# Six column groups of an SSD input projection with 512-column matmuls, and half of the gate columns moved one product later

## The chip, the core and the metric

The kernel runs on one core of a Trainium2 chip. The core has a matrix engine (TensorE, PE in the profile, with its weight loads shown apart as PEld), a vector engine (VectorE, DVE), a scalar engine (ScalarE, ACT), GpSimd (POOL, nearly unused here) and a queue (SyncE, SP) that issues the DMAs. Each engine works through its own queue in the order that was fixed when the program was built, and waits on semaphores for what others deliver. The metric is the device time of one launch in microseconds (us); less is better.

## What is computed

One sequence of 256 tokens passes through two layers of width 2048. Layer A is a Mamba-2 SSD mixer, layer B a dilated attention over keys and values made from layer A's output. In the reference, cut to layer A:

```python
shift, scale, gate = _adaln(c, ada_w[layer], ada_b[layer])
h = x * (1.0 + scale) + shift
proj = h @ in_w
z, xBC, dt = jnp.split(proj, [SSD_D_INNER, SSD_D_INNER + SSD_CONV_DIM], axis=-1)
xBC = jax.nn.silu(_causal_depthwise_conv(xBC, conv_w, conv_b))
xs, Bm, Cm = jnp.split(xBC, [SSD_D_INNER, SSD_D_INNER + SSD_BC_DIM], axis=-1)
...
y = _ssd_chunked(xs * dt[..., None], dt * A, Bm, Cm)
y = y + (xs * D_skip[:, None]).reshape(bsz, L, SSD_D_INNER)
y = y * jax.nn.silu(z.astype(jnp.float32))
...
return y @ out_w
...
x = _layer_norm(DEEPNORM_ALPHA * x + (1.0 + gate) * y, ln_g[layer], ln_b[layer])
```

`adaln` gives shift, scale and gate by the product of silu(c) with a matrix of 2048 x 6144. The input projection has 4096 columns for `z`, 4096 for `xs`, 1024 each for B and C, and 64 for `dt`. The heads fall into eight groups of 512 columns.

## The kernel before

**Precision.** Every operand of a large product is split in two: a high part, rounded to the type that the matrix engine multiplies, and the rest as a low part. Each product is the sum of high x high, high x low and low x high. `split` (L96) does that for a weight piece of 128 x 1024 numbers (512 KB): ACT copies `raw` to `whi` (L99), DVE subtracts to get `wlo` (L101). `load_piece` (L91) issues the DMA on SP; there are six `raw` buffers, and four each of `whi` and `wlo`. Layer A's input is kept as `hp` (L284), 128 x 2 x 16 x 256: first all 16 k tiles of the high part (`hhi`), then all of the low part (`hlo`).

**Forms of a product.** `cm_quad` (L132) makes 512 output columns, transposed, with the weights as the stationary operand: per piece two k tiles, per k tile and block of 128 columns three matmuls of 256 columns, in `cm_piece` (L125 to L127). Its four blocks share two PSUM tiles `acc`. `cm_wide` (L139), which layer B uses, makes 256 output columns: a high weight block is multiplied with both halves of the input side by side, 512 columns (L149), a low block with the high half, 256 columns (L152); the sums of the two halves lie next to each other in one `acc` tile per block, and are brought together by an ACT copy (L156) and a DVE addition (L157). `tm_chunk` (L181) makes 512 columns with tokens on the partitions (matmuls at L173 to L175). The pool `mm` holds four `acc` tiles in all.

**Layer A.** The input projection is cut into products named by kind and group: `bc` (B and C of two groups), `xs` and `z` of one group. Some of them are begun while h is still being made (`begun`, L310). In the loop at L628, turn g makes, in this order, `bc` of the next two groups (odd g), `xs` of group g + 1, the first SSD stage of group g (`stage1`), `z` of group g + 1, and the second SSD stage (`stage2`). Each of the four blocks of `xs` then passes `conv` (L316): ACT starts a sum (L320), DVE adds three shifted terms (L323), ACT applies SiLU (L325). For `xs` of groups 2 to 7 these read PSUM directly. Then follows the SSD output's product with `wout` in four parts of 512 columns (L720), 16 weight pieces each; under the first one y is transposed and split (`y_tiles`, L659). Each part ends with `residual` (L683), on DVE, which needs a piece of the gate row.

**The adaLN columns.** One column step loads 1 MB (`ada_load`, L242, tile `araw`, two buffers) and takes one DVE instruction of 2048 elements per partition (`ada_dot`, L251). `queue` (L267) puts such steps into the list `jobs`; each step also loads the next column. `background(n, every)` (L106) is called after every weight piece, and pops a job each time that its count reaches `every`. Layer A's 16 gate columns are queued in turn 1 of the loop, with one job for every five pieces (`R = (1, 5)`, L518), with `gate_out` (L258) behind them: bias, transpose on PE (L262), copy (L264), store to the DRAM row `gated` (L265). The first eleven columns for layer B are queued behind the first `wout` product (L727). `residual` reads the gate row by a broadcast DMA into `gt` (L730 and L731).

**Order.** The program is written as a sequence; a scheduler lays out each engine's queue by the written order and by when it expects operands and buffers to be ready, so an instruction can come ahead of its written place. Where the code has `tc.issue_after`, an instruction is held behind another on its engine.

Of the kernel before, what the change touches and what calls it, by code (L numbers as in the profile page):

```python
# [9 lines left out]
F32 = mybir.dt.float32  # L10
# [8 lines left out]
P = 128  # L19
L = 256  # L20
D = 2048
KT = D // P
# [24 lines left out]


@with_exitstack
def trunk(ctx, tc, xT, x, c, par, cst, bias, lnrow, ada, wdt, win, wout, wk, wv, wbin, wbout, out):  # L50
    nc = tc.nc
    V, S, T, PO = nc.vector, nc.scalar, nc.tensor, nc.gpsimd

# [82 lines left out]
            background(*rate)  # L136
        return ps

    def cm_wide(src, dst, rate=(0, 1)):  # L139


        ps = acc_pair()
        for q in range(KT // 4):
            hi, lo = (t.rearrange("p k n -> p (k n)").rearrange("p (k n) -> p k n", k=4)
                      for t in split(load_piece(src[q])))
            for k in range(4):
                kt = 4 * q + k
                for n in range(2):
                    T.matmul(ps[n], hi[:, k, n * P:n * P + P], xp[:, kt], start=kt == 0, stop=False,  # L149
                             skip_group_check=True)  # L150
                for n in range(2):
                    T.matmul(ps[n][:, 0, :], lo[:, k, n * P:n * P + P], xhi[:, kt, :], start=False, stop=kt == KT - 1,  # L152
                             skip_group_check=True)
            background(*rate)
        for n in range(2):
            S.activation(dst[:, n, :], ps[n][:, 1, :], AF.Copy)  # L156
            V.tensor_tensor(dst[:, n, :], ps[n][:, 0, :], dst[:, n, :], op=ALU.add)  # L157
# [132 lines left out]
    with ExitStack() as cA:  # L290
# [4 lines left out]
        def as_cm(t):  # L295
            return t.rearrange("p b n -> p (b n)").rearrange("p (i l) -> p i l", i=4)
# [8 lines left out]
        with ExitStack() as cS:  # L305
# [1 line left out]
            p0 = cS.enter_context(tc.tile_pool(name="p0", bufs=2))  # L307
            szt = [p0.tile([P, 2, 512], F32, name="sz") for _ in range(2)]

            begun = {("z", 0): (win[12], 6, szt[0]), ("z", 1): (win[13], 4, szt[1]),  # L310
                     ("xs", 1): (win[5], 4, as_cm(y[0])), ("bc", 2): (win[1], 4, as_cm(y[1])),
                     ("z", 2): (win[14], 14, y[2]), ("bc", 4): (win[2], 12, as_cm(y[3])), ("z", 4): (win[16], 6, y[4]),
                     ("bc", 6): (win[3], 12, as_cm(y[5])), ("z", 6): (win[18], 10, y[6]), ("z", 5): (win[17], 8, y[7])}
            xs, bc, sz = {}, {}, dict(enumerate(szt))

            def conv(ps, ct, dst):  # L316
# [24 lines left out]
            def hl_(kt):  # L341
                return hlo[:, kt, :]

            def product(kind, g, pre=None):

                src, k0, part = begun.get((kind, g), (None, 0, None))
                if src is None:
                    src = win[{"bc": g // 2, "xs": 4 + g, "z": 12 + g}[kind]]
                if kind == "z":
                    ps = tm_chunk(src, hh_, hl_, rate=R, k0=k0, pre=pre)  # L350
                    if g not in sz:
                        sz[g] = p0.tile([P, 2, 512], F32, name="sz")
                    for b in range(2):
                        if part is not None:
                            V.tensor_tensor(part[:, b, :], ps[b], part[:, b, :], op=ALU.add)
                        S.activation(sz[g][:, b, :], part[:, b, :] if part is not None else ps[b], AF.Silu)
                    return
                ps = cm_quad(src, hhi, hlo, rate=R, k0=k0)
                t = tiles(ps)
                if part is not None:  # L360
# [154 lines left out]
            aux = cS.enter_context(tc.tile_pool(name="aux", bufs=2, space=PSUM, reuse_waits="tile"))  # L515
            aux2 = cS.enter_context(tc.tile_pool(name="aux2", bufs=2, space=PSUM, reuse_waits="tile"))
            px = pe = cS.enter_context(tc.tile_pool(name="px", bufs=2, reuse_waits="tile"))
            R = (1, 5)  # L518


            scratch = wp1.tile([P, D], F32, name="araw")
# [106 lines left out]
            for g in range(G - 1):  # L628
                if g == 1:
                    pin[0] = latest[-1].ins  # L630
                    queue(wp1, [(0, "gate", kt) for kt in range(KT)])
                    jobs.append(lambda: gate_out(0))
                if g % 2 == 1:
                    product("bc", g + 1)
                product("xs", g + 1)
                if rs is not None:
                    stage3(g - 1, rs)
                st1 = stage1(g)
                if g < G - 2:
                    product("z", g + 1)  # L640
                rs = stage2(g, *st1)
# [71 lines left out]
        def first_weights(q):  # L713

            if q % 3 == 2 and q < 12:
                i = q // 3
                into = [slots.tile([P, 1024], F32R, name=f"s{2 * i + j}") for j in range(2)]
                first_v.append(split(load_piece(wv[2 * (i % 2)][i // 2]), into=into))

        for n in range(4):  # L720
            ps = tm_chunk(wout[n], lambda kt: yhi[kt // 16][:, kt % 16, :], lambda kt: ylo[kt // 4][:, kt % 4, :],
                          nk=2 * KT, rate=(1, 4) if n else (0, 1),
                          pre={0: y_ahead, 3: first_weights}.get(n), split_end=4 if n == 3 else 0)
            if n == 0:
                pin[0] = latest[-3].ins
                state[0] = 0
                queue(pn, cols1[:11])  # L727
            if n == 3:
                drain()
            gt = pn.tile([P, 512], F32, name="gt")  # L730
            bcast(gt, gated[0], 512 * n)  # L731
            for b in range(2):
                xr = pn.tile([P, 512], F32, name="xr", bufs=2)
                nc.sync.dma_start(xr, rows(x, b)[:, 512 * n:512 * n + 512])
                residual(n, ps[b], b, (gt, u[b][:, 512 * n:512 * n + 512]), xr)
                if n == 3:
# [86 lines left out]
    R = (0, 1)  # L823
# [192 lines left out]
def _dt(w):  # L1016

    a = np.zeros((2, 8, P, P), w.dtype)
    a[..., :64] = w.reshape(2, 8, P, 64)
    return a.transpose(0, 2, 1, 3).reshape(2, P, 1024)  # L1020


def _layout(x, c, ada_w, ada_b, ln_g, ln_b, a_in_w, a_conv_w, a_conv_b, a_dt_bias,
            a_A_log, a_D, a_norm_g, a_out_w, kv_w, b_in_w, b_out_w):
    f = np.float32
    par = np.zeros((P, NPAR), f)

# [36 lines left out]
    bc = np.stack([bb.reshape(D, G, P), cc.reshape(D, G, P)], 2).reshape(D, 2048)  # L1064
    win = _pieces(np.concatenate([bc, xs, z], 1))
    return {
        "xT": x[0].T.reshape(KT, P, L).transpose(1, 0, 2), "x": x[0], "c": c, "par": par, "cst": cst, "bias": bias,
        "lnrow": np.stack([ln_g[0], ln_b[0], ln_g[1], ln_b[1]]),
        "ada": ada, "wdt": _dt(dt), "win": win,
        "wout": _pieces(a_out_w[0]), "wk": _pieces(kv_w[:, :3072], 256, 4),  # L1070
        "wv": _pieces(kv_w[:, 3072:]), "wbin": _pieces(b_in_w[0], 256, 4), "wbout": _pieces(b_out_w[0]),
    }
# [20 lines left out]
```

## Time and profile before

| | |
|---|---|
| median of three runs | 1263.39 us (1263.02 to 1263.94) |
| the profiled execution | 1263.64 us, its span 1261.9 us |
| PE busy | 1225.5 us (97%) |
| DVE busy | 1023.6 us (81%) |
| ACT busy | 697.8 us (55%) |
| DMA | 335.92 MB, mean 266 GB/s |

All times inside the profile count from the start of the span. The busy time of an engine is the union of its instructions; matmuls are pipelined, so a matmul's shown length overlaps the next one, and distances between starts tell its price. "<-" in a wait names what ended it. The SSD loop with the rest of the input projection ends near 530 us; the four `wout` products follow.

### The profile page before, as it was taken

How to read it: one execution, taken by the hardware profiler on the slowest of the kernel's cores; microseconds unless marked ns; L12 is line 12 of the kernel's file. 1: busy time of each engine (PE TensorE's matmuls, PEld its weight loads, DVE VectorE, ACT ScalarE, POOL GpSimd, SP SyncE). 2: the span in 40 equal slices, each digit the busy share in tenths (PEclk: the TensorE clock that was granted, in tenths of full speed). 3: DMA queues.
4: the chain of work that ended last, by engine and by line, in shares of the span. 5: the costliest groups of instructions: out<-in, count | busy, mean ns of one | idle time of the engine just before them, and what ended most of it. 6: DMA issues, size and time to landing. Idle time of an engine off the chain costs nothing.

```text
span 1261.9 us, 19472 instructions
## 1 busy us (share of the span) xinstructions
PE 1225.5 (97%) x7470; PEld 1065.7 (84%) x7470; DVE 1023.6 (81%) x1442; ACT 697.8 (55%) x1017; POOL 0.2 (0%) x4
## 2 busy tenths in 40 slices
PE   4999999999999999999999999999999999999997
PEld 4889999899899989778888788888887888888886
DVE  6999986999998977869766579788888866758777
ACT  3655577857678876854344444334345644445631
POOL 0000000000000000000000000000000000000000
PEclk9999999999999999999999999999999999999999
DMA  9999968696876446568988469989998774364741
GB/s 379 422 421 423 420 237 282 217 338 252 311 272 216 161 152 208 184 213 315 322 286 280 151 189 350 359 331 343 355 381 324 247 238 149 120 196 132 227 179 66
DMA packets 80589, 335.92 MB, mean 266 GB/s; under 512 B 9104, under 2 KB 9328, under 8 KB 67696
## 3 DMA queue, kind: packets, MB, share of 16 engines
q1 hardware_dynamic: 80496, 334.69, 73.7%
q8 instruction: 58, 0.95, 0.3%
q14 instruction: 35, 0.29, 0.1%
HBM read 332.47 MB, written 2.18 MB: 265 GB/s over the span
## 4 chain that ended last, share of the span: by engine, by line
PE 80%; DVE 9%; DMA 6%; ACT 2%; issue 2%; SPq 0%; DVEq 0%; ACTq 0%
PE acc L149 13%; PE acc L175 12%; PE acc L174 12%; PE acc L173 12%; PE acc L127 7%; PE acc L125 7%; PE acc L152 7%; PE acc L126 6%; DMA araw<-in_ada 3%; DVE wlo L101 2%; DVE araw L251 2%; DVE cacc L323 1%; DMA raw<-in_wk 1%; DMA pT<-in_lnrow 1%; PE py L613 1%
## 5 line engine op out<-in xcount | busy, mean ns | idle before, releaser
L99 ACT ACTIVATE whi<-raw 128x1024 fp32r<-128x1024 f32 x392 | 411.6, 1058 | 376.6 <-PE acc L175 125.0
L101 DVE TENSOR_TENSOR wlo<-raw,whi 128x1024 fp32r<-128x1024 f32 x392 | 474.2, 1223 | 148.6 <-ACT whi L99 144.6
L149 PE MATMUL acc<-actT,whi 128*128 128x512 f32 x896 | 284.2, 397 | 0.0
L174 PE MATMUL acc<-wlo,actT 128*128 128x512 f32 x688 | 269.8, 392 | 1.0 <-DVE wlo L101 0.8
L173 PE MATMUL acc<-whi,actT 128*128 128x512 f32 x688 | 266.9, 394 | 0.5 <-ACT actT L670 0.5
L125 PE MATMUL acc<-actT,whi 128*128 128x256 f32 x768 | 218.2, 286 | 17.6 <-ACT actT L402 17.5
L251 DVE SCALAR_TENSOR_TENSOR araw<-araw,cb__72 128x2048 f32<-128x2048 f32 x96 | 219.6, 2288 | 17.5 <-DMA araw<-in_ada 17.4
L127 PE MATMUL acc<-actT,wlo 128*128 128x256 f32 x768 | 215.9, 286 | 5.8 <-DVE wlo L101 5.8
L126 PE MATMUL acc<-actT,whi 128*128 128x256 f32 x768 | 217.7, 285 | 0.0
L152 PEld LDWEIGHTS acc<-actT,wlo 128*128 128x128 f32 x896 | 166.8, 188 | 43.2 <-DVE wlo L101 5.6
L152 PE MATMUL acc<-actT,wlo 128*128 128x256 f32 x896 | 178.1, 280 | 2.1 <-DVE wlo L101 1.7
L175 PE MATMUL acc<-whi,actT 128*128 128x512 f32 x432 | 168.8, 391 | 0.0
L125 PEld LDWEIGHTS acc<-actT,whi 128*128 128x128 f32 x768 | 148.5, 194 | 19.3 <-ACT actT L402 17.7
L174 PEld LDWEIGHTS acc<-wlo,actT 128*128 128x128 f32 x688 | 129.3, 188 | 28.9 <-DVE wlo L101 3.3
L127 PEld LDWEIGHTS acc<-actT,wlo 128*128 128x128 f32 x768 | 147.2, 194 | 7.1 <-DVE wlo L101 6.6
L173 PEld LDWEIGHTS acc<-whi,actT 128*128 128x128 f32 x688 | 128.7, 188 | 26.6 <-ACT actT L670 1.2
L126 PEld LDWEIGHTS acc<-actT,whi 128*128 128x128 f32 x768 | 148.9, 194 | 0.3
L149 PEld LDWEIGHTS acc<-actT,whi 128*128 128x128 f32 x896 | 137.4, 189 | 0.2
L175 PE MATMUL acc<-whi,ylo 128*128 128x512 f32 x256 | 100.2, 392 | 0.0
L175 PEld LDWEIGHTS acc<-whi,actT 128*128 128x128 f32 x432 | 81.1, 188 | 16.7
L175 PEld LDWEIGHTS acc<-whi,ylo 128*128 128x128 f32 x256 | 48.0, 188 | 9.7
L323 DVE SCALAR_TENSOR_TENSOR cacc<-acc,prm,cacc 128x253 f32<-128x253 f32 (+2 forms) x96 | 42.1, 477 | 4.6 <-ACT cacc L320 4.4
(253 smaller groups left out, 1051.9 us busy)
## 6 DMA issues: line engine op xcount, KB each, us to landing
araw<-in_ada SPq DMA_DIRECT2D x96, 1024.0 KB, 7.7
raw<-in_win SPq DMA_DIRECT2D x160, 512.0 KB, 5.5
raw<-in_wout SPq DMA_DIRECT2D x64, 512.0 KB, 4.7
raw<-in_wbin SPq DMA_DIRECT2D x64, 512.0 KB, 4.3
raw<-in_wv SPq DMA_DIRECT2D x48, 512.0 KB, 5.7
raw<-in_wk SPq DMA_DIRECT2D x48, 512.0 KB, 8.3
cbc<-cumd SPq DMA_DIRECT2D x16, 512.0 KB, 5.4
raw<-in_wbout SPq DMA_DIRECT2D x16, 512.0 KB, 4.1
```

The costliest lines, as they stand in the source:

```text
L99: copied.append(S.activation(hi, raw, AF.Copy))
L101: latest.append(V.tensor_tensor(lo, raw, hi.bitcast(F32), op=ALU.subtract))
L125: T.matmul(o, hi[:, k, c_], ahi[:, kt, :], start=first, stop=False, skip_group_check=True)
L126: T.matmul(o, hi[:, k, c_], alo[:, kt, :], start=False, stop=False, skip_group_check=True)
L127: T.matmul(o, lo[:, k, c_], ahi[:, kt, :], start=False, stop=kt == k1 - 1, skip_group_check=True)
L149: T.matmul(ps[n], hi[:, k, n * P:n * P + P], xp[:, kt], start=kt == 0, stop=False, skip_group_check=True)
L152: T.matmul(ps[n][:, 0, :], lo[:, k, n * P:n * P + P], xhi[:, kt, :], start=False, stop=kt == KT - 1, skip_group_check=True)
L173: T.matmul(o, h_, hi[:, k, :], start=kt == k0, stop=False, skip_group_check=part)
L174: T.matmul(o, h_, lo[:, k, :], start=False, stop=False, skip_group_check=part)
L175: end = T.matmul(o, l_, hi[:, k, :], start=False, stop=kt == k1 - 1, skip_group_check=part)
L251: V.scalar_tensor_tensor(raw, raw, 1.0, cb_, op0=ALU.mult, op1=ALU.mult, accum_out=mod[layer][:, ct, j:j + 1])
L323: V.scalar_tensor_tensor(acc[:, o:], ps[:, :L - o], w[:, j:j + 1], acc[:, o:], op0=ALU.mult, op1=ALU.add)
```

## The change

Two parts of layer A change. First, `xs` of groups 2 to 7 is made by `cm_wide`, twice per group with 256 columns each, from weights that lie in an array of their own (`wxs`, pieces of 512 KB that hold four k tiles of 256 columns). `cm_wide` gets its moving operand as a parameter: `hp[:, :, kt, :]` for both halves, two runs of 256 columns. Each of its four results lies in SBUF in the tile `xs`, and `conv` works on it in place; the first two blocks of a group are convolved as soon as the first half of the product is done. `win` loses these columns, so the index of the `z` columns in it moves down by six.

Second, of the 16 gate columns the first eight stay in the SSD loop, with one job for every ten pieces; the other eight and `gate_out` are queued ahead of the first `wout` product, in the pool `pn`, with one job for every two pieces, and what is left of them is drained behind that product, ahead of its residual.

```diff
-    def cm_wide(src, dst, rate=(0, 1)):
+    def cm_wide(src, dst, rate=(0, 1), moving=None):
+        both, high = moving or (lambda kt: xp[:, kt], lambda kt: xhi[:, kt, :])
...
-                    T.matmul(ps[n], hi[:, k, n * P:n * P + P], xp[:, kt], start=kt == 0, stop=False,
+                    T.matmul(ps[n], hi[:, k, n * P:n * P + P], both(kt), start=kt == 0, stop=False,
...
-                    T.matmul(ps[n][:, 0, :], lo[:, k, n * P:n * P + P], xhi[:, kt, :], start=False, stop=kt == KT - 1,
+                    T.matmul(ps[n][:, 0, :], lo[:, k, n * P:n * P + P], high(kt), start=False, stop=kt == KT - 1,
...
+            def xs_wide(g):
+                xs[g] = p0.tile([P, 4, L], F32, name="xs")
+                for w in range(2):
+                    t = xs[g][:, 2 * w:2 * w + 2, :]
+                    cm_wide(wxs[2 * g - 4 + w], t, rate=R, moving=(lambda kt: hp[:, :, kt, :], hh_))
+                    for n in range(2):
+                        conv(t[:, n, :], 4 * g + 2 * w + n, t[:, n, :])
+
             def product(kind, g, pre=None):
+                if kind == "xs" and g > 1:
+                    return xs_wide(g)
...
-            R = (1, 5)
+            R = (1, 10)
...
-                    queue(wp1, [(0, "gate", kt) for kt in range(KT)])
-                    jobs.append(lambda: gate_out(0))
+                    queue(wp1, [(0, "gate", kt) for kt in range(KT // 2)])
...
+        state[0] = 0
+        queue(pn, [(0, "gate", kt) for kt in range(KT // 2, KT)])
+        jobs.append(lambda: gate_out(0))
         for n in range(4):
             ps = tm_chunk(wout[n], lambda kt: yhi[kt // 16][:, kt % 16, :], lambda kt: ylo[kt // 4][:, kt % 4, :],
-                          nk=2 * KT, rate=(1, 4) if n else (0, 1),
+                          nk=2 * KT, rate=(1, 4) if n else (1, 2),
                           pre={0: y_ahead, 3: first_weights}.get(n), split_end=4 if n == 3 else 0)
             if n == 0:
+                drain()
                 pin[0] = latest[-3].ins
...
-    win = _pieces(np.concatenate([bc, xs, z], 1))
+    win = _pieces(np.concatenate([bc, xs[:, :1024], z], 1))
...
+        "ada": ada, "wdt": _dt(dt), "win": win, "wxs": _pieces(xs[:, 1024:], 256, 4),
```

Left out are the new argument `wxs` of `trunk`, the renumbering of `win` in `begun` and `product`, and unchanged lines.

More of the change, by code (lines that the diff above doesn't have):

```diff
@@ L49, in trunk @@
 @with_exitstack
-def trunk(ctx, tc, xT, x, c, par, cst, bias, lnrow, ada, wdt, win, wout, wk, wv, wbin, wbout, out):
+def trunk(ctx, tc, xT, x, c, par, cst, bias, lnrow, ada, wdt, win, wxs, wout, wk, wv, wbin, wbout, out):
     nc = tc.nc
@@ L308, in trunk @@
             szt = [p0.tile([P, 2, 512], F32, name="sz") for _ in range(2)]
-            begun = {("z", 0): (win[12], 6, szt[0]), ("z", 1): (win[13], 4, szt[1]),
+            begun = {("z", 0): (win[6], 6, szt[0]), ("z", 1): (win[7], 4, szt[1]),
                      ("xs", 1): (win[5], 4, as_cm(y[0])), ("bc", 2): (win[1], 4, as_cm(y[1])),
-                     ("z", 2): (win[14], 14, y[2]), ("bc", 4): (win[2], 12, as_cm(y[3])), ("z", 4): (win[16], 6, y[4]),
-                     ("bc", 6): (win[3], 12, as_cm(y[5])), ("z", 6): (win[18], 10, y[6]), ("z", 5): (win[17], 8, y[7])}
+                     ("z", 2): (win[8], 14, y[2]), ("bc", 4): (win[2], 12, as_cm(y[3])), ("z", 4): (win[10], 6, y[4]),
+                     ("bc", 6): (win[3], 12, as_cm(y[5])), ("z", 6): (win[12], 10, y[6]), ("z", 5): (win[11], 8, y[7])}
             xs, bc, sz = {}, {}, dict(enumerate(szt))
@@ L342, in hl_ @@
                 return hlo[:, kt, :]
+            def xs_wide(g):
[5 more added lines that the diff above has]
+                        conv(t[:, n, :], 4 * g + 2 * w + n, t[:, n, :])
             def product(kind, g, pre=None):
+                if kind == "xs" and g > 1:
+                    return xs_wide(g)
                 src, k0, part = begun.get((kind, g), (None, 0, None))
                 if src is None:
-                    src = win[{"bc": g // 2, "xs": 4 + g, "z": 12 + g}[kind]]
+                    src = win[{"bc": g // 2, "xs": 4 + g, "z": 6 + g}[kind]]
                 if kind == "z":
@@ L1068, in _layout @@
         "lnrow": np.stack([ln_g[0], ln_b[0], ln_g[1], ln_b[1]]),
-        "ada": ada, "wdt": _dt(dt), "win": win,
+        "ada": ada, "wdt": _dt(dt), "win": win, "wxs": _pieces(xs[:, 1024:], 256, 4),
         "wout": _pieces(a_out_w[0]), "wk": _pieces(kv_w[:, :3072], 256, 4),
```

## The prediction

> **What bounds the kernel now.** I read the page's head and its chain first, then the busy time of each engine by stage, then the waits of TensorE in layer A, and last the order of single instructions around the change.
>
> ```profile
> span 1261.9 us, 19472 instructions
> ...
> PE 80%; DVE 9%; DMA 6%; ACT 2%; issue 2%; SPq 0%; DVEq 0%; ACTq 0%
> ```
>
> ```profile
> 236.00:400.00 164.00, 161.36 (x1285) 150.09 (x1284) 158.84 (x242) 121.50 (x197) 0.00 (x0) 1.00 0.79 281
> 400.00:531.50 131.50, 128.45 (x1035) 114.89 (x1033) 109.87 (x196) 101.03 (x169) 0.00 (x0) 0.99 0.54 179
> 531.50:581.00 49.50, 49.32 (x242) 39.58 (x242) 38.71 (x63) 29.33 (x48) 0.00 (x0) 1.00 0.71 239
> 581.00:625.00 44.00, 44.00 (x195) 36.43 (x195) 34.34 (x34) 16.99 (x16) 0.00 (x0) 1.00 0.94 343
> ```
>
> The columns are the stretch, its length, then busy time of PE, PEld, DVE, ACT and POOL, the granted clock, the DMA share and GB/s. From 236 to 531.5 us (SSD loop, the rest of the input projection) PE is busy 289.8 of 295.5 us. It sets the end here. But DVE is busy 158.84 of 164 us in the first of these stretches: it could not follow a much faster PE. The third row is nearly the first product of the SSD output (`wout[0]`), the fourth the second one.
>
> ```profile
> PE acc L127 <- DVE wlo L101: 3.8, 3, 2.1
> ```
>
> That is the longest entry among PE's waits between 216 and 531.5 us: three waits for the low half of a weight split, 3.8 us in total, one of 2.1 us. So two things can be won in this stage: matmul time itself, and a few microseconds behind DVE.
>
> **The matmuls of groups 2 to 7.** Before, each of the 16 k tiles of a group takes 12 matmuls of 256 columns; after, 4 of 512 and 4 of 256 (hi weights against h's halves side by side, lo weights against the high half). The columns, 3072, stay. Both forms stand in the trace, the second in layer B's projections.
>
> ```profile
> 302.11 0.28 PE L125 MATMUL acc<-actT,whi 128*128 128x256 f32 x1
> ...
> 314.59 0.28 PE L127 MATMUL acc<-actT,wlo 128*128 128x256 f32 x1
> ```
>
> ```profile
> 804.62 0.63 PE L149 MATMUL acc<-actT,whi 128*128 128x512 f32 x2
> 805.09 0.39 PE L152 MATMUL acc<-actT,wlo 128*128 128x256 f32 x2
> ...
> 814.37 0.63 PE L149 MATMUL acc<-actT,whi 128*128 128x512 f32 x2
> ```
>
> Starts are what count, since the ends are modelled. From 302.11 to 314.59 there are 104 steps: 0.120 us for 256 columns. From 804.62 to 814.37 there are 14 k tiles of two column blocks: 0.696 us for each. A group took 192 x 0.120 = 23.04 us and will take 32 x 0.696 = 22.28 us: 0.76 us less, **4.5 us** for six groups.
>
> One thing differs from layer B: there both halves of a k tile lie side by side, here they are two runs of 256 columns far apart in `hp`. No row shows such a moving operand. Bounds: nothing, or at most that the break costs as much as a second matmul, which makes 512 columns 0.240 us and the gain nil. I take nothing, because the 0.120 us repeat for every instruction of 256 columns, whatever it reads, and so look like a price of the instruction.
>
> The Trainium skill ("TensorE: Matmul & The Clock Gate", section Back-to-back issue gap) puts an isolated warm gap at N/2.4 + 2.5 ns, 109 ns for 256 columns and 216 ns for 512; the trace has 120, and 0.47/2 = 235 ns. By the page 64 matmuls fewer are worth 0.16 us per group, an estimate of 1.0 us in all. The measurement decides, but that result stands below as a rival.
>
> **What the wide form adds.** Each of 24 column blocks (4 in each of six groups) gets an ACT copy out of PSUM and a DVE add, rows of layer B:
>
> ```profile
> L156 ACT ACTIVATE s<-acc x20: 364/380/384, 797.9 to 900.2; 128x256 f32<-128x256 f32 x20
> ```
>
> ```profile
> L157 DVE TENSOR_TENSOR s<-acc,s x20: 414/418/428, 799.2 to 900.6; 128x256 f32<-128x256 f32 x20
> ```
>
> ACT: 24 x 0.380 = 9.1 us; it has 295.5 - 222.5 = 73 us idle in the stage, so nothing on the path. DVE: 24 x 0.418 = 10.0 us. In the stretch to 400 us not even half of that would fit, if nothing left it (5.1 us idle). Weight pieces stay at 8 of 512 KB per group, so splits and DMAs are as many as before; the smaller `win` and the new `wxs` cost nothing, since the same bytes arrive by the same queue. PSUM: the two halves of a group take the four `acc` banks in turn, two at a time; the first half's banks are asked for again only after the second half, 11.1 us later. The tightest case is behind group 2, where `z` 2 has a single piece left, and there the add has to wait for two blocks only, where before the next product waited for convolutions reading PSUM. I cost it at nothing; without that cover it is one eviction, 0.8 us.
>
> **What leaves the SSD loop.** Eight of the 16 gate columns.
>
> ```profile
> L251 DVE SCALAR_TENSOR_TENSOR araw<-araw,cb__72 x16: 2283/2291/2303, 239.4 to 398.6; 128x2048 f32<-128x2048 f32 x16
> ```
>
> That is 8 x 2.29 = 18.3 us off DVE, and 8 MB off SP's queue. The net on DVE in the stage is 10.0 - 18.3 = -8.3 us. The sixteen ran between 239 and 401 us, well ahead of the pace that the rate of 1 in 5 writes down (the last is called in product `z` 7), so the new rate of 1 in 10 will not space them either: the eight will come early, and the relief falls after about 310 us. The early waits, 1.7 of the 3.8 us, I leave in place.
>
> **The stall at 472 us.** This is where the order of the convolutions matters. Chain of waits, then the stretches around it:
>
> ```profile
> 460.57 2.33 DVE cacc L323 x6
> ...
> 471.36 1.15 DVE wlo L101
> 472.50 0.04 issue
> 472.55 0.39 PE acc L127
> ```
>
> ```profile
> 472.00:474.00 2.00, 1.46 (x10) 1.46 (x11) 2.00 (x3) 1.99 (x2) 0.00 (x0) 0.90 0.70 262
> 474.00:476.00 2.00, 2.00 (x11) 2.00 (x11) 2.00 (x4) 1.44 (x5) 0.00 (x0) 0.50 0.84 274
> 476.00:478.00 2.00, 2.00 (x15) 2.00 (x15) 1.39 (x3) 1.84 (x4) 0.00 (x0) 0.75 0.83 281
> ```
>
> Behind group 6's product DVE has four convolutions (12 steps of 2.33/6 = 0.39 us) beside the SSD work of group 5, and reaches the next low half late. PE stands 2.1 us, and then the granted clock falls: 2 x 0.10 + 2 x 0.50 + 2 x 0.25 = 1.7 us more. In the wide form the first two blocks are convolved under the second half's matmuls, and only two convolutions and two adds remain behind the product: 6 x 0.39 - 2 x 0.418 = 1.5 us less DVE work ahead of that weight. The wait shrinks to some 0.6 us, and the clock may hold. Bounds: the whole 3.8 us, or a loss of 1 us if the adds queue elsewhere as these did. I take **2.5 us** gained.
>
> The Trainium skill ("TensorE: Matmul & The Clock Gate", section Why this matters for your kernels) has the clock fall only after an idle gap of more than about 3 us; here it fell after 2.1 us. By the page a new stall of 2 us would cost only itself, by the trace 3.8 us; the trace decides.
>
> **What comes into the first SSD output product.** Eight columns (one per two weight pieces), then the gate's bias, transpose, copy, store, and the first broadcast of the gate row.
>
> ```profile
> L251 DVE SCALAR_TENSOR_TENSOR araw<-araw,cb__72 128x2048 f32<-128x2048 f32 x3 | 6.9, 2289 | 0.0
> ```
>
> DVE's group of that name between 531.5 and 581 us: three columns of layer 1, which now come later. DVE's room there is 49.5 - 38.71 + 6.9 = 17.7 us, the newcomers take 18.3: full to 0.6 us. In the next stretch it has 9.7 us left, enough for the three.
>
> ```profile
> 528.05 0.42 SPq L244 DMA_DIRECT2D araw<-in_ada  x1
> ...
> 537.26 0.42 SPq L244 DMA_DIRECT2D araw<-in_ada  x1
> ```
>
> ```profile
> araw<-in_ada SPq DMA_DIRECT2D x96, 1024.0 KB, 7.7
> ...
> gt<-gated SPq DMA_DIRECT2D x4, 256.0 KB, 6.0
> ```
>
> ```profile
> DMA to landing us min/median/max: 1.3/2.3/3.3
> ```
>
> ```profile
> 581.50 1.28 DVE L685 TENSOR_TENSOR u<-acc,gt 128x512 f32<-128x512 f32 x2
> ...
> 585.09 2.35 DVE L101 TENSOR_TENSOR wlo<-raw,whi 128x1024 fp32r<-128x1024 f32 x2
> ```
>
> The landing times belong to the store of the gate row; the last two rows are the residual of this product, which starts when PE is done with it, and the first low half behind it. The two column buffers of this pool were first loaded at 528 and 537 us; a buffer then needs 7.7 + 2.3 + 0.4 = 10.4 us per turn. The eighth column, fourth in the second buffer, ends at 537.3 + 3 x 10.4 + 10.0 = 578.5 us. The transpose comes behind the product on PE, near 581; half a microsecond later, copied, the row goes out, and is back in `gt` at 581.5 + 2.3 + 6.0 = 590 us. So the residual starts some 8 us later than at 581.50, and DVE runs in order: low halves for the second product stand behind it. The one at 585.09 is the fourth piece's; its matmuls are due three pieces (12 matmuls at 0.235 = 2.8 us each) after 581, at 589.4. If the order leaves it behind the late residual, it is ready at 590 + 3.6 + 1.2 = 594.8: 5.4 us of stall, and 1.7 for the clock. If two more splits go ahead of the residual, nothing is lost. Bounds 0 and 7.1 us. SP waits too, for the copied row and for the store; weights behind it are up to six loads ahead and cover that. I take **2.5 us** lost, nearer to zero, because the order is made with the loads' times counted in.
>
> **Sum.** -4.5 - 2.5 + 2.5 = -4.5 us on the profiled execution's 1263.64 us (span 1261.9): 1259.1. That execution stands 0.25 us above the median of the runs, so the forecast is 1258.9 us.
>
> **Rivals.**
>
> A, no matmul time is won (the two runs count as two matmuls, or the gap is the page's, which leaves 1.0 us): -2.5 + 2.5 to -1.0 on top, 1262.4 to 1263.4 us, taken as 1262.9. For it: no row has the operand. Against: 0.120 us in hundreds of rows.
>
> B, slower: the transpose of the gate columns holds PE. It is one instruction in PE's queue; if the order expects the eighth column earlier than it lands, all matmuls behind it stand.
>
> ```profile
> 455.71 0.27 PE L262 MATMUL aux<-cc,mod 128*16 128x128 f32 x1
> ```
>
> ```profile
> DVE araw L251 <- DMA araw<-in_ada: 17.4, 13, 7.0
> ```
>
> For it: in the old order this transpose, written behind product `z` 7, ran at 455.7 us, so it does go ahead of its place; and DVE does wait for columns expected too early. Against: without the 7.0 us at the very start these are 12 waits of 0.9 us. If each load were counted a third short of its 7.7 us, the fourth in its buffer would be expected 4 x 2.6 = 10.3 us early; with 1.7 for the clock, in place of the 2.5: -7.0 + 12.0 = +5.0, 1268.4 us. It decides from 7.0 us on.
>
> C, DVE becomes the bound of the SSD loop: the early eight columns with the adds of groups 2 to 4 fill 158.84 + 5.0 of 164 us before any relief, and PE gives back what it won; the stall at 472 us, after the relief, still shrinks: 1263.4 - 2.5 + 2.5 = 1263.4 us. For it: that stretch's row. Against: the columns are placed where DVE is idle, and eight fewer come.
>
> **Chances.** A difference of 0.2% (2.5 us) is about what a measurement of this kernel can tell from no change. Forecast 0.62 (own range 1254.5 to 1261.5; all but 0.04 of it faster), A 0.08 (no change), C 0.13 (0.08 no change, 0.03 slower, 0.02 faster), B 0.17 (slower, but 0.02). Faster 0.60, no change 0.22, slower 0.18. The range runs from all of the stall's 3.8 us won and nothing lost (1263.4 - 8.3 = 1255.1) to short of B's price, 1265.5, with half a microsecond below for waits that I left in place.
>
> **What would show it.** Right: L125, L126 and L127 at 384 matmuls each, L149 and L152 at 1280, 0.696 us per k tile in the new rows; the loop's end near 524 us instead of 531.5; no half clock near 470 us; column dots between 536 and 579 us. Wrong: 512-column starts 0.24 us apart or more; PE's longest wait at L262 or behind L685; DVE over 97% from 236 to 500 us.

## The result and the profile after

The changed kernel takes 1254.7 us (median of six runs, 1252.97 to 1255.17) beside 1262.69 us for the kernel before on the same chip (six runs, 1261.64 to 1263.94). The ratio is 0.9935 [0.9925, 0.9946]: 8.0 us faster. The forecast was 4.5 us faster; the measured time lies in the range, near its lower end.

The page's head and the chain that ended last, of the changed kernel:

```profile
span 1252.5 us, 18746 instructions
...
PE 86%; DVE 5%; DMA 5%; issue 2%; ACT 1%; SPq 0%; DVEq 0%; ACTq 0%
```

PE's share of the chain rose from 80 to 86%, DVE's fell from 9 to 5%: the chain is the same, with fewer pieces in which PE waits for DVE. The stretches, with borders that follow the earlier end of the loop (columns as before):

```profile
236.00:400.00 164.00, 164.00 (x1092) 142.22 (x1091) 152.84 (x253) 127.40 (x216) 0.00 (x0) 1.00 0.69 239
400.00:522.50 122.50, 119.16 (x840) 99.32 (x838) 108.66 (x191) 99.14 (x172) 0.00 (x0) 1.00 0.54 178
522.50:572.00 49.50, 49.17 (x243) 39.76 (x244) 47.63 (x75) 29.37 (x49) 0.00 (x0) 1.00 0.92 332
572.00:616.00 44.00, 44.00 (x197) 36.32 (x196) 34.94 (x35) 16.99 (x16) 0.00 (x0) 1.00 0.95 360
```

In the first stretch PE has no idle time left, where it had 2.64 us. In the third, DVE is busy 47.63 of 49.50 us with the late gate columns, and PE is busy 49.17 us of it (49.32 before). PE's longest wait for DVE between 216 and 523 us, of those after:

```profile
PE acc L152 <- DVE wlo L101: 2.1, 1, 2.1
```

So the early waits are gone, and a wait of 2.1 us is there as before (it starts near 465 us). One wait has grown, for ACT, at the start of the first output product; before and after:

```profile
PE acc L173 <- ACT actT L670: 0.3, 1, 0.3
PE acc L173 <- ACT actT L681: 1.2, 1, 1.2
```

It comes with the wide form: it stands at 1.2 us in every profile that has it, and isn't there with the moved columns alone. Why ACT is later there wasn't tried. The starts of the wide form's matmuls, from PE's timeline in group 7:

```profile
445.05 0.63 PE L149 MATMUL acc<-actT,whi 128*128 128x512 f32 x2
...
449.23 0.63 PE L149 MATMUL acc<-actT,whi 128*128 128x512 f32 x2
```

Six k tiles of two blocks in 4.18 us: 0.697 us for each, as in layer B. The two runs of 256 columns far apart cost nothing that this shows.

**Where the time came from.** The loop is best added up over PE's records: from the first matmul of `stage2` of group 0 (L604 before, L616 after) to the first transpose of y (L666, L677). "Matmuls" is the number of instructions of each kind by its distance between starts; "idle" is the time without any matmul record; "half clock" is half the time for which the profile shows the granted clock at 0.50. All in us, one line per profiled execution; the experiments' rows are used further down.

```
kernel, execution        length  matmuls  idle  half clock  waits of PE over 0.3 us, and when
before                    297.9   287.2    5.1     1.7      1.35 @246, 0.42 @253, 0.88 @373, 2.08 @472, 0.37 @516
before, again             296.2   287.2    4.9     0        1.38 @248, 0.45 @254, 0.65 @374, 2.08 @474, 0.37 @516
changed                   288.8   282.7    2.1     0        2.08 @467
changed, again            290.3   282.7    2.1     1.7      2.08 @467
changed, third            288.8   282.7    2.1     0        2.08 @467
without the late eight    288.8   282.7    2.1     0        2.07 @467
wide form alone           294.5   282.8    6.0     1.7      1.38 @247, 0.97 @289, 2.67 @295, 1.03 @473
wide form alone, again    295.4   282.8    6.7     1.7      1.40 @247, 0.97 @289, 2.68 @295, 0.62 @376, 1.03 @474
moved columns alone       296.6   287.1    3.1     3.4      2.61 @508, 0.51 @509
moved columns, again      295.4   287.1    3.4     1.7      2.62 @507, 0.74 @509
all sixteen late          288.8   282.7    2.1     0        2.07 @469
split ahead               287.1   282.7    0.5     0        0.49 @469
ahead and held            287.2   282.7    0.5     0        0.50 @469
```

The loop became 9.1 us shorter between the two first executions: 4.5 of matmuls, 3.0 of idle time, 1.7 of half clock. The span became 9.4 us shorter, so on balance nearly all of it is in the loop; behind it, 1.7 us of half clock in the kernel before (near 716 us) stand against the longer wait for ACT, 0.9 us, and small differences in the rest. (The 3.9 to 4.0 us that the terms leave over are starts that come later than the usual distance, with no time free of a matmul record; they are the same in both. Without any use of the distances, as length less idle time and half clock, the loop went from 291.1 and 291.3 us in the two profiles before to between 286.5 and 286.7 in the three after.)

### The profile page after: what moved, and what is told of

Its sections match the earlier page's. It is cut to its first block, busy times and chain, and to the rows that moved or that the text cites. A ratio compares the mean times of both kernels' runs of the same rounds, so it can differ in the third digit from the quotient of the medians.

```text
span 1252.5 us, 18746 instructions
## 1 busy us (share of the span) xinstructions
PE 1218.5 (97%) x7086; PEld 1042.7 (83%) x7086; DVE 1032.4 (82%) x1466; ACT 702.1 (56%) x1039; POOL 0.2 (0%) x4
## 4 chain that ended last, share of the span: by engine, by line
PE 86%; DVE 5%; DMA 5%; issue 2%; ACT 1%; SPq 0%; DVEq 0%; ACTq 0%
PE acc L149 20%; PE acc L174 13%; PE acc L175 13%; PE acc L173 13%; PE acc L152 10%; PE acc L125 3%; PE acc L127 3%; PE acc L126 3%; DMA raw<-in_wk 2%; DVE wlo L101 1%; PE py L625 1%; DMA raw<-in_win 1%; DVE araw L251 1%; DMA araw<-in_ada 1%; DMA raw<-in_wv 1%
## 5 line engine op out<-in xcount | busy, mean ns | idle before, releaser
L149 PE MATMUL acc<-actT,whi 128*128 128x512 f32 x1280 | 405.2, 397 | 0.0
L152 PE MATMUL acc<-actT,wlo 128*128 128x256 f32 x1280 | 253.7, 280 | 4.5 <-DVE wlo L101 3.7
L149 PEld LDWEIGHTS acc<-actT,whi 128*128 128x128 f32 x1280 | 195.8, 189 | 0.4
L125 PE MATMUL acc<-actT,whi 128*128 128x256 f32 x384 | 108.9, 288 | 17.6 <-ACT actT L414 17.5
L126 PE MATMUL acc<-actT,whi 128*128 128x256 f32 x384 | 109.5, 287 | 0.0
L127 PE MATMUL acc<-actT,wlo 128*128 128x256 f32 x384 | 107.3, 287 | 1.2 <-DVE wlo L101 1.2
L125 PEld LDWEIGHTS acc<-actT,whi 128*128 128x128 f32 x384 | 74.3, 194 | 18.6 <-ACT actT L414 17.7
L126 PEld LDWEIGHTS acc<-actT,whi 128*128 128x128 f32 x384 | 75.1, 196 | 0.3
L583 ACT ACTIVATE seg<-cbc,cumT 128x128 f32<-128x128 f32 x128 | 41.2, 389 | 5.0 <-PE py L625 4.9
```

The costliest lines, as they stand in the source:

```text
L125: T.matmul(o, hi[:, k, c_], ahi[:, kt, :], start=first, stop=False, skip_group_check=True)
L126: T.matmul(o, hi[:, k, c_], alo[:, kt, :], start=False, stop=False, skip_group_check=True)
L127: T.matmul(o, lo[:, k, c_], ahi[:, kt, :], start=False, stop=kt == k1 - 1, skip_group_check=True)
L149: T.matmul(ps[n], hi[:, k, n * P:n * P + P], both(kt), start=kt == 0, stop=False, skip_group_check=True)
L152: T.matmul(ps[n][:, 0, :], lo[:, k, n * P:n * P + P], high(kt), start=False, stop=kt == KT - 1, skip_group_check=True)
L583: S.activation(seg[:, hh, b, :], cbc[:, hh, b, :], AF.Relu, bias=cumT[:, b, h0 + hh:h0 + hh + 1], scale=-1.0)
```

## The experiments

Every kernel is an edit of the changed one, unless it is said otherwise. Times are medians with the lowest and highest run; the kernel before ran beside them on the same chip.

**The wide form alone.** All gate columns go back into the loop, with the old rate.

```diff
-            R = (1, 10)
+            R = (1, 5)
-                    queue(wp1, [(0, "gate", kt) for kt in range(KT // 2)])
+                    queue(wp1, [(0, "gate", kt) for kt in range(KT)])
+                    jobs.append(lambda: gate_out(0))
...
-        state[0] = 0
-        queue(pn, [(0, "gate", kt) for kt in range(KT // 2, KT)])
-        jobs.append(lambda: gate_out(0))
-                          nk=2 * KT, rate=(1, 4) if n else (1, 2),
+                          nk=2 * KT, rate=(1, 4) if n else (0, 1),
-                drain()
```

> The wide xs alone; all 16 gate columns stay in the SSD loop at one job in five pieces, as before. Theory 1 (the terms add up): the 4.5 us of matmul starts come off whatever DVE does, and the two waits near 246 and 252 us (1.8 us of PE idle) stay, since the early columns are as they were: 4.0 to 5.5 us under before, near 1258. Theory 2 (coupled): with 10 us more on a DVE that is 97% busy from 236 to 400 us the PE gives the gain back, 0 to 2 us under before, and the waits of PE behind L101 grow from 3.8 us.

Measured: 1260.8 us (1258.05 to 1263.46, 11 runs) beside 1261.76, ratio 0.9987 [0.9976, 0.9998]. The matmuls give their 4.4 us, and 1.0 us of it in this profile, 1.9 in the later one, comes back as waits in the loop. The chain of waits of this kernel:

```profile
291.39 1.38 DVE s L367 x2
292.76 0.60 DVE s L627
293.36 0.60 DVE s L626
293.96 1.14 DVE wlo L101
...
295.15 0.50 PE acc L152 x2
```

and its stretches just behind:

```profile
236.00:300.00 64.00, 58.98 (x412) 52.34 (x411) 63.58 (x97) 48.62 (x81) 0.00 (x0) 0.97 0.75 275
...
297.00:299.00 2.00, 2.00 (x9) 1.71 (x7) 2.00 (x3) 0.91 (x5) 0.00 (x0) 0.50 0.93 219
```

DVE is full to 300 us (63.58 of 64.00), with the additions of the wide form on top of seven columns, and PE is idle for 5.0 us there (1.8 before). At 293.96 the low half that PE needs comes behind `z`'s addition (L367) and two steps of `stage2` (L626, L627). PE stands 2.7 us, and the clock is halved behind it. This is rival C in part, for this half of the change alone: the loop keeps some of what it won.

**The moved columns alone.** `xs_wide` isn't called, and `win` is whole again.

```diff
-                if kind == "xs" and g > 1:
-                    return xs_wide(g)
...
-                    src = win[{"bc": g // 2, "xs": 4 + g, "z": 6 + g}[kind]]
+                    src = win[{"bc": g // 2, "xs": 4 + g, "z": 12 + g}[kind]]
...
-    win = _pieces(np.concatenate([bc, xs[:, :1024], z], 1))
+    win = _pieces(np.concatenate([bc, xs, z], 1))
```

Left out is the renumbering of `win` in `begun`.

> The gate columns' move alone; xs stays in matmuls of 256 columns. Theory 1: the waits of PE behind DVE at 246, 252 and 373 us (about 3 us with what they drag) go, and the first output product costs nothing: 2.5 to 4 us under before, near 1259.5. Theory 2 (coupled): they go only together with the wide form, whose other order of loads and columns removed them: 0 to 1.5 us under before. The forecast's own row (2.5 us lost in the output product, waits left) would give 2.5 us over before.

Measured: 1260.84 us (1259.54 to 1264.26, 12 runs), ratio 0.9996 [0.9987, 1.0006]: no difference. Yet all the waits of before are gone, the one near 472 us too. Another has come, in this list of waits:

```profile
PE py L623 <- DVE seg L584: 2.6, 1, 2.6
```

with these stretches behind it:

```profile
509.00:511.00 2.00, 1.98 (x4) 0.50 (x4) 2.00 (x5) 2.00 (x4) 0.00 (x0) 0.50 0.00 0
511.00:513.00 2.00, 2.00 (x19) 1.76 (x19) 2.00 (x5) 0.35 (x1) 0.00 (x0) 0.50 0.29 59
```

The output of an SSD stage waits 2.6 us for the decay factors (`seg`), and the clock stays halved for two windows in this execution. Why the order comes out so in this kernel wasn't tried.

**All sixteen columns late.** None in the loop, all under the first output product, one per weight piece.

```diff
-                    queue(wp1, [(0, "gate", kt) for kt in range(KT // 2)])
+                    pass
...
-        queue(pn, [(0, "gate", kt) for kt in range(KT // 2, KT)])
+        queue(pn, [(0, "gate", kt) for kt in range(KT)])
-                          nk=2 * KT, rate=(1, 4) if n else (1, 2),
+                          nk=2 * KT, rate=(1, 4) if n else (1, 1),
```

> The changed kernel with all 16 gate columns under the first output product, one per piece. DVE's ledger there: 17.7 us of room against 16 x 2.29 = 36.6 us. If that ledger bounds, PE loses part of the 19 us that are over, 6 to 19 us more than the changed kernel (1261 to 1274), with PE waiting behind L101 or the transpose at L262; if the columns slide into the second product, whose DVE has 9.7 us of room, and the late gate row is covered by splits put ahead of it, under 3 us more. The SSD loop itself then shows what the remaining eight columns cost it.

Measured: 1281.01 us (1278.49 to 1282.45, 4 runs), ratio 1.015 [1.0135, 1.0165]. The loop is as long as the changed kernel's to 0.1 us (288.8): the eight columns that stayed in it cost nothing there. Behind it the waits of PE pile up:

```profile
PE aux L677 <- DVE ylo L682: 7.8, 5, 2.6
PE acc L174 <- DVE wlo L101: 4.6, 7, 1.6
...
PE aux L262 <- DVE mod L256: 1.6, 1, 1.6
```

```profile
572.00:616.00 44.00, 32.65 (x117) 23.75 (x118) 38.70 (x44) 11.32 (x13) 0.00 (x0) 0.84 0.86 318
```

The last wait shown is rival B's, the transpose L262 that holds PE. The stretch below the list is one in which the changed kernel has PE busy for all 44.00 us. By the two spans it is 28.2 us slower than the changed kernel, and 1.7 of them lie ahead of the loop, which starts at 232.3 instead of 230.6 us. The rest adds up: eight more columns of 2.29 us are 18.3 us, since the first eight already fill DVE's 17.7 us of room, and five windows of half clock in this execution (17 us in all) cost 8.5 more: 26.8 us.

**Without the late eight columns.** The price of what the first output product took in. The kernel leaves the eight columns out and sets their sums to zero, so half of the gate is missing from its result.

```diff
-        queue(pn, [(0, "gate", kt) for kt in range(KT // 2, KT)])
+        V.memset(mod[0][:, KT // 2:, 2:3], 0.0)
```

> The changed kernel without the eight late gate columns: their loads and dots are left out and their sums set to zero, so the gate is wrong for half of the columns; gate_out stays behind the first output product. If the eight cost nothing there, the time is the changed kernel's within 1 us; if DVE's full queue costs the 2.5 us of the forecast, it is 2 to 3 us less.

Measured: 1253.99 us (1253.37 to 1254.39, 5 runs), ratio 0.9935 [0.9922, 0.9948]. In this stretch DVE has its room back, and PE's busy time is the same to 0.03 us:

```profile
522.50:572.00 49.50, 49.14 (x243) 39.12 (x242) 38.24 (x66) 28.82 (x49) 0.00 (x0) 1.00 0.72 233
```

From the first transpose of y to layer B's first matmul of 512 columns (L149), by PE's records, it takes 256.7 us; the three profiles of the changed kernel have 256.2 to 256.5. So no profile of the changed kernel shows a price of the late columns.

**The kernels again.** The changed kernel and the one before, unchanged, on the chip of that run.

> The changed kernel once more, on the chip of its neighbours: 8 us under before (7 to 9). A second profile: the loop's length near 288.8 us and its one long wait at 467 us should come again, since the order is fixed; windows of half clock may fall elsewhere.

> The kernel before once more, for a second profile: the same waits of PE at 246, 252, 373 and 472 us to 0.3 us, since the order is fixed. If the half clock follows from the length of the wait alone, it comes again at 473 and 716 us; if it is a matter of where a wait falls in a window that runs by itself, it comes at other waits, and this explains why the runs of this kernel lie 6.6 us apart.

Measured: changed 1256.59 us (1253.21 to 1257.12, 5 runs), ratio 0.9948 [0.9935, 0.9962]; before 1262.17 us in one run. Without the late eight columns the kernel is 2.6 us faster than this on the same chip, and 1.2 us faster than all 17 runs of the changed kernel together, in three measurements (median 1255.17). The profiles show no loss of PE to the late columns. Part of the difference is the clock: the five runs without the columns show a granted clock of 0.9988 in the mean, the five beside them 0.998, which is 1.0 us of the span. Whether the columns cost the rest, in some executions and not in others, isn't shown. What these two runs bring is the half clock. The same wait of 2.08 us stands in both kernels and all executions, and now it is the changed kernel that has the half clock behind it:

```profile
466.00:468.00 2.00, 0.72 (x3) 0.72 (x4) 2.00 (x4) 1.98 (x3) 0.00 (x0) 0.84 0.48 195
468.00:470.00 2.00, 2.00 (x8) 1.61 (x7) 2.00 (x2) 2.00 (x7) 0.00 (x0) 0.50 0.79 221
```

and the kernel before doesn't:

```profile
472.00:474.00 2.00, 0.29 (x2) 0.29 (x3) 2.00 (x3) 1.98 (x5) 0.00 (x0) 1.00 0.27 51
474.00:476.00 2.00, 2.00 (x19) 2.00 (x19) 2.00 (x3) 1.99 (x5) 0.00 (x0) 1.00 0.77 217
```

**One split written ahead.** The first weight piece of group 7 is split ahead of `stage2` of group 5, so that DVE meets its low half before that stage's work.

```diff
-                      for t in split(load_piece(src[q])))
+                      for t in (w0 if w0 is not None and q == 0 else split(load_piece(src[q]))))
...
+                if g == 5:
+                    ahead[7, 0] = split(load_piece(wxs[10][0]))
                 rs = stage2(g, *st1)
```

Left out is how `xs_wide` hands the piece on to `cm_wide` as `w0`.

> The changed kernel, with the first weight piece of xs of group 7 split one step earlier in the written order, ahead of the second SSD stage of group 5. If the wait of 2.08 us at 467 us is DVE serving that stage and the z addition first, it goes, with no other: 1.5 to 2.5 us under the changed kernel, and no half clock behind it in any run. If the wait is DVE's whole backlog, it moves to the next weight piece or into the stage, and the time stays within 1 us.

Measured: 1254.3 us (1251.29 to 1255.96, 6 runs), ratio 0.9936 [0.9923, 0.9949]. The wait of 2.08 us shrinks to 0.49, and the loop is 1.7 us shorter; but the runs spread more. The profiled execution is the slowest of them, and its chain of waits has the reason, in the first output product:

```profile
527.96 2.22 DVE araw L251 x2
...
530.20 7.79 DMA araw<-in_ada
...
538.09 2.30 DVE araw L251 x2
540.39 0.41 DVE ylo L687
...
540.84 0.44 PE aux L682 x2
```

DVE stands idle for 2.36 us until the third late column's 1 MB has landed, and a low part of y, which PE needs, stands behind it: PE is idle for 2.0 us up to 540.8, and a half clock follows, 3.7 us in all. The order of these instructions is the same in the changed kernel, where the column came 0.37 us late in the first profile and in time in the other two.

**Split ahead, and the late columns held.** As above, and the late columns start two pieces later, each from the third on held behind the split of its piece (`latest`, `pin`), so that the order can't bring one ahead.

```diff
+            if hold and i > 1:
+                pin[0] = latest[-1].ins
             ada_dot(*cols[i], raw)
...
-        state[0] = 0
-        queue(pn, [(0, "gate", kt) for kt in range(KT // 2, KT)])
+        state[0] = -2
+        queue(pn, [(0, "gate", kt) for kt in range(KT // 2, KT)], hold=True)
```

> The changed kernel with the early split of the run before, and with the third and later of the late gate columns two weight pieces further back, each held behind the low half that stands before it. In the run of the early split alone DVE waited 7.8 us for the third late column, PE stood 2.0 us behind it at 541 us and the clock halved; in the changed kernel's own profiles the same column came just in time. If that column decides the spread of the runs, this kernel's runs lie within 3 us of each other, and its median is 2 to 4 us under the changed kernel on the same chip; if the spread comes from elsewhere, it is within 1.5 us of the early split's 2.3 us gain.

> The changed kernel, as the neighbour of the next two on one chip: 6.5 to 8.2 us under before, as in the two measurements so far; the loop without the clock's part 288.7 us.

Measured: 1251.95 us (1251.39 to 1254.86, 5 runs), ratio 0.9922 [0.9909, 0.9935]. The changed kernel on the same chip took 1255.19 us (1252.85 to 1255.88, 6 runs), ratio 0.994 [0.9927, 0.9952]. Four of the five runs lie below all six of the changed kernel: it beats both kernels, by some 3 us the one that was to be explained. In DVE's timeline of this kernel the column now comes behind the parts of y, with no idle time before it:

```profile
538.79 0.87 DVE L689 SCALAR_TENSOR_TENSOR ylo<-aux,prm,actT 128x256 fp32r<-128x256 f32 x2
539.57 2.29 DVE L251 SCALAR_TENSOR_TENSOR araw<-araw,cb__72 128x2048 f32<-128x2048 f32 x1
```

**The two halves again,** on this chip, since the first results lay so near to no change.

> The wide xs alone, again. Additive theory: its loop without the clock's part is 292.8 us again (3.4 us under before's 296.2), and its median 2.5 to 4 us under before; the 1.6 us of the first measurement were then more half-clock windows at its longer waits (2.7 us at 295 us). Coupled theory: 1 to 2 us under before again.

> The move alone, again. Additive theory: its loop without the clock's part is 293.2 us again (3.0 us under before), its median 2 to 3.5 us under before. Coupled theory: within 1 us of before again, with half-clock windows behind its 2.6 us wait at 507 us in the profile.

Measured: wide form alone 1259.84 us (1256.76 to 1261.7, 12 runs), ratio 0.9978 [0.9969, 0.9987]; moved columns alone 1260.31 us (1259.23 to 1262.3, 12 runs), ratio 0.9985 [0.9974, 0.9996], beside 1262.27. By the ratios the halves bring 1.6 and 0.5 us on the first chip, 2.8 and 1.9 here; both together bring 6.6 to 8.2. The table of the loop says why. With the half clock taken off, the loop is 296.2 us long before, 292.8 and 293.7 in the wide form alone, 293.2 and 293.7 with the moved columns alone, 288.6 to 288.8 with both: 2.5 to 3.4, 2.5 to 3.0, and 7.5 us. That is 1.1 to 2.5 us more than the sum. The rest goes with the half clock: each half alone has a wait of 2.6 to 2.7 us, and in all four profiles a half clock behind it. In the runs it weighs with the moved columns above all: their granted clock is 0.9963 in the mean of 24 runs, beside 0.9972 in 46 of the kernel before and 0.9978 in 17 of the changed one, and 0.001 of it is 1.3 us of the span. The wide form alone has 0.9972 in 23 runs; what it loses behind the loop is the 0.9 us of the longer wait for ACT.

## Why the prediction was right in its direction, and wrong in its size

**Matmuls, -4.5 us: right.** 287.2 to 282.7 us in the loop, 0.697 us per k tile; the profiles show 4.4 to 4.8 us without the distances. Rival A falls with it.

**What the wide form adds, nothing: right only together with the other half.** The 24 additions cost PE nothing in the changed kernel, whose first stretch has PE at 164.00 of 164.00 us. With all sixteen columns early they cost it the waits of the experiment with the wide form alone. The prediction saw that DVE had no room for them unless columns left, but expected that relief only after about 310 us; it came from 243 us on. That the form adds nothing isn't quite right either: the wait for ACT at the start of the first output product is 0.9 us longer with it, and the prediction has no term for that.

**"The early waits, 1.7 of the 3.8 us, I leave in place": this step failed.** All went, and with them the two waits that I hadn't counted: 1.35 + 0.42 + 0.88 + 0.37 = 3.0 us. These two, in the list of before:

```profile
PE aux L582 <- DVE cb L561: 0.9, 1, 0.9
PE acc L174 <- DVE wlo L101: 0.4, 1, 0.4
```

So the term was put at nothing, and it was 3.0 us. I looked at how many columns run early, and not at where the second one stands. DVE's timeline before:

```profile
242.90 2.30 DVE L251 SCALAR_TENSOR_TENSOR araw<-araw,cb__72 128x2048 f32<-128x2048 f32 x1
...
245.18 1.24 DVE L101 TENSOR_TENSOR wlo<-raw,whi 128x1024 fp32r<-128x1024 f32 x1
...
246.38 1.24 DVE L101 TENSOR_TENSOR wlo<-raw,whi 128x1024 fp32r<-128x1024 f32 x1
...
249.09 2.29 DVE L251 SCALAR_TENSOR_TENSOR araw<-araw,cb__72 128x2048 f32<-128x2048 f32 x1 [1.40 <-DMA araw<-in_ada]
```

and after:

```profile
243.08 1.22 DVE L101 TENSOR_TENSOR wlo<-raw,whi 128x1024 fp32r<-128x1024 f32 x1
...
244.29 1.22 DVE L101 TENSOR_TENSOR wlo<-raw,whi 128x1024 fp32r<-128x1024 f32 x1
...
245.49 2.29 DVE L251 SCALAR_TENSOR_TENSOR araw<-araw,cb__72 128x2048 f32<-128x2048 f32 x1
```

Before, the second column (2.30 us) stands ahead of two low halves that PE is about to need, and ahead of the next low half DVE stands idle for 1.40 us until the third column's load has landed. After, both low halves go first, and there is no idle time. The wide form alone, with sixteen columns at the old rate, keeps the wait at 247 us (1.38 us); the moved columns alone lose it. So for this wait it is the columns, not the matmuls. Whether it is their number or the rate of one in ten wasn't taken apart.

**The stall at 472 us, -2.5 us: wrong in its mechanism.** I took it that the convolutions hold the low half back, and that fewer of them shorten the wait by 1.5 us. It is 2.08 us in both kernels. The chain of the changed kernel:

```profile
463.92 1.38 DVE s L367 x2
465.30 0.60 DVE s L626
465.89 1.14 DVE wlo L101
467.08 0.50 PE acc L152 x2
```

Two convolutions fewer, and the low half is as late as ever: the addition of `z` 6 (L367) and a step of `stage2` of group 5 (L626) stand ahead of it in DVE's order. The chain of before has the same work there, between the convolutions and the low half; I passed over it:

```profile
467.76 0.60 DVE s L355
...
470.67 0.69 DVE s L614
471.36 1.15 DVE wlo L101
```

With the moved columns alone all four convolutions are there, and the wait is gone all the same; with the wide form alone it is 1.03 us. So its length goes with the order that comes out, not with the number of convolutions. One split moved in the written order takes 1.6 of the 2.08 us away. The other 1.7 us, the half clock, did go in the first profile; but it comes and goes with the execution (behind this wait in 2 of 7 profiles, once in either kernel), so it is no gain of the change.

**The first output product, +2.5 us: the delay is right, its price was mis-sized.** DVE's timeline after:

```profile
573.91 0.27 DVE L264 COPY row<-aux 16x128 f32<-16x128 f32 x1
...
580.80 1.22 DVE L101 TENSOR_TENSOR wlo<-raw,whi 128x1024 fp32r<-128x1024 f32 x1
581.94 1.28 DVE L696 TENSOR_TENSOR u<-acc,gt 128x512 f32<-128x512 f32 x2
```

The residual's first instruction starts at 581.94 us. In the kernel without the late columns it starts 8.2 us sooner, as this line's first start shows:

```profile
L696 DVE TENSOR_TENSOR u<-acc,gt x8: 680/683/691, 573.7 to 704.7; 128x512 f32<-128x512 f32 x8
```

By the trace the gate row's broadcast lands at 581.4 us, so its way through DRAM delays the residual by what was forecast (8 us). But the order put the low halves ahead of it, the last at 580.80, and PE is busy 44.00 of 44.00 us from 572 on. That is the lower bound of 0 that the prediction gave; I took 2.5 between it and 7.1. A price shows in one profile only, with the split ahead, where the third column's load lands late: 3.7 us. How often that happens in the changed kernel isn't shown.

**Rivals.** B (the transpose holds PE) shows up only with all sixteen columns late, for 1.6 us. C (DVE becomes the bound) shows up only in the wide form alone, and there in part.

**The sum, by what the runs show:** -4.5 (matmuls) - 3.0 (idle time in the loop) + 0.9 (the wait for ACT behind it) + 0 (late columns) = -6.6 us without the half clock; the loop alone is -7.5, and -9.1 or -5.9 with the half clock as it falls in two pairs of profiles. The medians say -8.0, the ratios of the three measurements -6.6 to -8.2. The forecast of -4.5 had its matmul term right, and its other two cancelled where the runs show -3.0 and 0.9. That the time still fell into the range is in part luck: the gain at 472 us that didn't come and the loss in the output product that didn't come were put at the same size.

## What to carry to other kernels

A wait of the engine that sets the end is read in the order of the engine that it waits for: which instruction stands ahead of the needed one, and would that still stand there with less work queued? Two halves of a change that load and unload the same engine are costed together; by the times, each half alone was worth 0.5 to 2.8 us, and both together 6.6 to 8.2. Where a late result has other work written ahead of it, the delay is free, and the price is to be looked for in what stands behind a wait for a load in the same queue.

## What the runs showed of the hardware

Whether the half clock comes behind a wait depends on where the wait falls as well as on its length. Behind PE waits of 2.07 to 2.08 us it came in 2 of 7 profiles, behind 2.6 to 2.7 us in 4 of 4, and behind a wait of 0.96 to 0.98 us at the start of layer B in 2 of 13. It lasts 3.4 us a time (or twice that), and costs 1.7 us each. In every profile the changes of the clock lie on one grid of 3.41 us. PE's records, cut by that grid from 216 to 1235 us in all 13 profiles, show this: each of the eleven windows in which PE is busy 41% of the time or less is followed by half clock. The others all have PE busy for some 50% or more, and four of them are followed by it: two of 64%, those with the wait of 0.98 us, and two that were at half clock themselves. Why these four count isn't shown. The wait of 2.08 us lies whole in one window in the two profiles that have half clock behind it (PE busy 39%), and across a border in the other five (53% or more in either window).

The waits themselves repeat to within some 0.3 us from execution to execution, since the order is fixed, and the runs' spread goes with the clock: of the 17 runs of the changed kernel the five with a granted clock of 0.999 took 1252.85 to 1254.55 us, the seven with 0.996 or 0.997 took 1255.09 to 1257.12.

The Trainium skill ("TensorE: Matmul & The Clock Gate", section What's actually happening) describes a window of about 3.4 us that runs by itself and decides over the clock by how busy PE was in it. The grid and the share of busy time agree. That a whole idle window is needed, as its table has it, does not: here windows in which PE was busy 39% were enough.

A moving operand of two runs of 256 columns far apart costs what one run of 512 does: 0.697 us per k tile here, 0.696 in layer B.
